# A decoder layer on one core: who makes the first product's scales, and in what order ScalarE and VectorE work within one of its blocks

## The chip, the cores and the metric

The kernel runs on one core of one Trainium2 chip. The metric is device time in microseconds (us) of one execution. Small values are better. TensorE (PE in the profile) multiplies matrices, VectorE (DVE) and ScalarE (ACT) work elementwise, GpSimd (POOL) sums over partitions, and nearly all loads are issued in order by SyncE's queue (SP).

## The reference, cut to what matters

```python
mod = (silu(c) @ w_ada + b_ada).reshape(B, 6, D)          # c: (1, 2048), w_ada: (2048, 6*2048)
sh1, sc1, gt1, sh2, sc2, gt2 = mod[:, j]                   # one row of 2048 each
h = rmsnorm(x, g_norm_mix) * (1.0 + sc1) + sh1             # x: (1, 512, 2048)
proj = h @ w_in                                            # w_in: (2048, 5120)
q, k, v, xr, xg = split(proj, 1024 columns each)
o_attn = stick_breaking_attention(q, k, v)                 # 8 heads of 128
o_lru  = rg_lru(conv(xr)) * gelu(xg)
x = x + gt1 * (concat(rmsnorm(o_attn), rmsnorm(o_lru)) @ w_out)
h = rmsnorm(x, g_norm_mlp) * (1.0 + sc2) + sh2
x = x + gt2 * (square(relu(h @ w_mlp_in)) @ w_mlp_out)     # hidden width 8192
return rmsnorm(x, g_norm_final)
```

All tensors are float32. The change lies in the first lines: silu(c), sc1 and the product that makes xr.

## The kernel before

**Layout.** x is kept transposed: 16 blocks `xs[k]` of 128 channels by 512 tokens. Every float32 product is done as three single-pass products in the format `float32r`: an operand is split into a high part `h` (a ScalarE copy into `float32r`) and a low part `lo` (VectorE: full minus high, in the helper `low`, line 123), and `mm3` (lines 266, 269, 270) adds high weights by high x, high weights by low x and low weights by high x.

**Before the first product.** The row c is loaded in two halves. The first half is broadcast by the load itself to all 128 partitions of `cb[0]` (512 KB written, 4 KB read 128 times). The second half lands on one partition (`crow`), and two matmuls in full float32 with a column of ones (line 182) put it on all partitions. ScalarE applies Silu to each. 12 matmuls into an unused bank follow (`WARM`, line 186).

**Modulation rows.** A row of `mod` for channel block j of kind m (`Rows.row(m, j)`) is a dot product of 128 rows of `w_ada` with silu(c): two tiles of 128x1024 are loaded, and VectorE makes one multiply pass over each that also adds up (line 216; each is followed by a short read of the accumulator). For the first product's kind `SC1`, VectorE then adds the two sums and the bias (line 225, into `mods`), and makes the scale gm1[k] = (sc1 + 1) * g_norm_mix (line 387).

**The first product** makes xr: for k = 0..15 it multiplies x[k] * gm1[k] with two 512-column halves of `w_in`, accumulating in all 8 PSUM banks, 24 matmuls of 512 columns for each k. The rsqrt factor of the norm and the shift are applied later, so the product can start before the sum of squares is known. Block k is prepared one k ahead: `weights1(k+1)` loads two weight halves into `wr` (4 buffers) and splits them, `load_x(k+j)` loads x of a later block and squares it (ScalarE), adding the square to `acc` (VectorE, line 369), and `prep1(k+1)` makes the row, the scale and the split of the scaled x: high on ScalarE (line 390), low on VectorE (line 391). When all 16 squares are in `acc`, GpSimd sums them over partitions (`rnorm_steps`, line 343), and ScalarE and VectorE make the rsqrt factor `r1` (lines 352 to 361).

**The second product** (q, k and v of two and four heads) uses the full norm: `prep2(k)` needs the row `SH1` of block k, `r1`, and splits again (lines 397, 399, 400). It needs the same 8 banks; ScalarE first copies the first product's results out of them (line 459).

**Order.** A scheduler orders each engine's instructions by priority, raised for some by `tc.high_priority(offset=...)`; instructions given to `later` (`tc.keep_in_program_order`) stand among each other in program order. All engines run their lists strictly in order.

Of the kernel before, what the change touches and what calls it, by code (L numbers as in the profile page):

```python
# [10 lines left out]
F32 = mybir.dt.float32  # L11
# [32 lines left out]
PAD, SHIFT = 8, 16  # L44
WARM = 12

# [19 lines left out]
def hybrid_layer_kernel(  # L66
# [87 lines left out]
    def triangles():  # L154
# [20 lines left out]
    crow = T("tt")  # L175
    nc.sync.dma_start(crow[0:1, :1024], c[:, 1024:])
    nc.sync.dma_start(cb[0], c[:, :1024].broadcast_to([P, 1024]))
    act(cb[0], cb[0], AF.Silu)
    for i in range(2):
        v = slice(i * S, (i + 1) * S)  # L180
        ps = bank("mm")
        later(mm(ps, ones[0:1, :], crow[0:1, v], start=True, stop=True))
        act(cb[1][:, v], ps, AF.Silu)
    warm = bank("o")
# [6 lines left out]
    class Rows:  # L191
# [15 lines left out]
        def row(self, m, j, tags, q=None):  # L207
# [4 lines left out]
            for q_ in (0, 1) if q is None else (q,):  # L212
                if (i, q_) not in self.tiles:
                    self.load(2, tags)
                t = self.tiles.pop((i, q_))
                ins = stt(
                    out=t, in0=t, scalar=1.0, in1=cb[q_], op0=ALU.mult, op1=ALU.mult, accum_out=self.ga[:, q_ : q_ + 1],
                )
                if q is not None or tags is MID:
                    later(ins)  # L220
                del t
                if tags is not MID:
                    self.load(1, tags)
            if q != 0:
                stt(
                    out=mod(m, j), in0=self.ga[:, 0:1], scalar=self.ga[:, 1:2], in1=col(C_BADA, i), op0=ALU.add, op1=ALU.add,
                )
# [109 lines left out]
    def rnorm(*args):  # L337
        return list(rnorm_steps(*args))[1]

    def rnorm_steps(accs, n, ptag, tok=slice(0, S), r=None):  # L340
        m = T("n")[:, tok]
# [14 lines left out]
        if ptag is None:  # L356
            later(ins)
        act(r, r, AF.Exp, scale=-0.5)
        tt(out=m, in0=m, in1=r, op=ALU.mult)
# [14 lines left out]
    xs, xhl, hT = {}, {}, {}  # L374

    def load_x(k):
        xs[k] = T("a")
        with tc.high_priority(offset=XPRI):
            ins = nc.sync.dma_start(xs[k], xT[blk(k), :])
            if k == 0:  # L380
                later(ins)
        add_square(acc, xs[k], T("n"), k == 0)

    def prep1(k, tags):
        rows.row(SC1, k, tags)
        g = gm1[:, k : k + 1]
        stt(out=g, in0=mod(SC1, k), scalar=1.0, in1=col(C_GMIX, k), op0=ALU.add, op1=ALU.mult)
        h, lo = T("a", F32R), T("a", F32R)
        with tc.high_priority(offset=RPRI if k > NK - 4 else 0):
            act(h, xs[k], AF.Copy, scale=g)  # L390
            stt(out=lo, in0=xs[k], scalar=g, in1=f32(h), op0=ALU.mult, op1=ALU.subtract)
        xhl[k] = h, lo

    def prep2(k):
        rows.row(SH1, k, EARLY)
        t = xs[k]
        stt(out=t, in0=t, scalar=gm1[:, k : k + 1], in1=r1, op0=ALU.mult, op1=ALU.mult)
        h, lo = T("a", F32R), T("a", F32R)
# [24 lines left out]
    load_x(0)  # L423
    w = weights1(0, [0])
    prep1(0, None)
    w += weights1(0, [1])
    load_x(1)
    rows.load(2, EARLY)
    for k in range(NK):
        if k + 1 < NK:  # L430
            w_next = weights1(k + 1)
            for j in (2,) if k < 4 else (2, 3) if k == 4 else (3,) if k < 8 else (3, 4) if k == 8 else (4,):
                if k + j < NK:
                    load_x(k + j)
# [1049 lines left out]
def _layout(inputs):  # L1484
# [39 lines left out]
```

## Time and profile before

| | |
|---|---|
| median of 3 runs | 1973.74 us (1971.24 to 1974.24) |
| the profiled execution, its own time | 1972.66 us |
| its span from first to last instruction | 1970.9 us |
| mean granted TensorE clock | 0.997 |
| busy over the span: PE, DVE, ACT, POOL | 98%, 89%, 54%, 10% |
| first matmul of the first product | 11.82 us after the span's start |
| first matmul of the second product | 106.38 us |

The profile is of one execution, with all times from the span's start. Start to start, successive 512-column matmuls stand 0.23 us apart at full clock, so a block of 24 takes 5.44 us; a matmul's own row says 0.39 us because matmuls overlap in the pipeline. An idle time in a row is that of the engine just before it, with the instruction that ended the wait. In the window tables the last three columns are the granted clock of TensorE, the mean busy share of the 16 DMA engines and the rate in GB/s.

### The profile page before, as it was taken

The numbers are of one execution on the slowest core, as the hardware profiler recorded it, in microseconds if no ns is written. First come the engines' busy times: TensorE is split into PE (matmuls) and PEld (weight loads), VectorE is DVE, ScalarE is ACT, GpSimd is POOL, SyncE is SP. The second block draws the span as 40 slices with busy tenths as digits, with TensorE's granted clock in tenths as the row PEclk, the third lists the DMA queues.
The fourth block names the chain that finished last, engine by engine and source line by source line (L and its number), as shares of the span: only waits on it lengthen the run. The fifth ranks groups of instructions, "written<-read, shape, count | busy, mean of one in ns | idle before, by whom it ended". The sixth has DMA issues, their size and how long they took to land. (4 is left out here: it accounts for less than half of the span.)

```text
span 1970.9 us, 37264 instructions
## 1 busy us (share of the span) xinstructions
PE 1936.0 (98%) x14184; PEld 1816.2 (92%) x14184; DVE 1756.5 (89%) x2972; ACT 1067.9 (54%) x1575; POOL 203.4 (10%) x325
## 2 busy tenths in 40 slices
PE   9999999999999999999999999999999999999997
PEld 7788888788888999999999999999999999999996
DVE  8998777878998589999999999999989879879897
ACT  4443564786533376565565555556445545646452
POOL 0000000000000001112112111200001210311110
PEclk9999999999999999999999999999999999999999
DMA  9987647545879545556656666765678668669553
GB/s 366 328 293 236 205 132 230 177 129 182 290 248 372 180 144 177 188 185 225 204 178 218 206 193 193 232 209 174 226 276 288 249 244 280 224 247 356 205 198 113
DMA packets 204086, 443.51 MB, mean 225 GB/s; under 512 B 20481, under 2 KB 42113, under 8 KB 203906
## 3 DMA queue, kind: packets, MB, share of 16 engines
q1 hardware_dynamic: 176338, 356.58, 54.5%
q0 software_dynamic: 25120, 82.33, 11.3%
q8 instruction: 111, 1.82, 0.4%
q10 hardware_dynamic: 2448, 2.21, 0.3%
q14 instruction: 69, 0.57, 0.1%
HBM read 376.30 MB, written 64.75 MB: 224 GB/s over the span
## 5 line engine op out<-in xcount | busy, mean ns | idle before, releaser
L1144 PE MATMUL ps_mm<-a,w 128*128 128x256 f32 x1680 | 463.3, 276 | 2.4 <-DVE a L1164 1.8
L1146 PE MATMUL ps_mm<-a,w 128*128 128x256 f32 x1680 | 464.0, 276 | 0.3 <-DVE w L123 0.3
L1145 PE MATMUL ps_mm<-a,w 128*128 128x256 f32 x1680 | 463.7, 276 | 0.3 <-DVE a L123 0.3
L1082 ACT ACTIVATE w<-raw 128x768 fp32r<-128x768 f32 x242 | 203.6, 842 | 297.7 <-issue 97.8
L1145 PE MATMUL ps_z<-a,w 128*128 128x256 f32 x1292 | 356.9, 276 | 0.9 <-DVE a L123 0.9
L1146 PE MATMUL ps_z<-a,w 128*128 128x256 f32 x1292 | 356.7, 276 | 0.2 <-DVE w L123 0.2
L1144 PE MATMUL ps_z<-a,w 128*128 128x256 f32 x1292 | 356.7, 276 | 0.1
L123 DVE TENSOR_TENSOR w<-ts,w 128x1024 fp32r<-128x1024 f32 x242 | 295.2, 1220 | 59.4 <-PE ps_z L1146 21.6
L1088 ACT ACTIVATE w<-ts 128x1024 fp32r<-128x1024 f32 x242 | 256.1, 1058 | 156.7 <-DVE ts L1084 141.1
L1144 PEld LDWEIGHTS ps_mm<-a,w 128*128 128x128 f32 x1680 | 315.0, 188 | 3.1 <-issue 2.9
L1146 PEld LDWEIGHTS ps_mm<-a,w 128*128 128x128 f32 x1680 | 315.4, 188 | 0.9 <-DVE w L123 0.9
L1145 PEld LDWEIGHTS ps_mm<-a,w 128*128 128x128 f32 x1680 | 315.4, 188 | 0.5 <-DVE a L123 0.5
L123 DVE TENSOR_TENSOR w<-raw,w 128x768 fp32r<-128x768 f32 (+2 forms) x296 | 267.5, 905 | 26.6 <-ACT w L249 23.1
L1145 PEld LDWEIGHTS ps_z<-a,w 128*128 128x128 f32 x1292 | 242.5, 188 | 1.4 <-DVE a L123 1.3
L1146 PEld LDWEIGHTS ps_z<-a,w 128*128 128x128 f32 x1292 | 242.5, 188 | 0.4 <-DVE w L123 0.4
L1144 PEld LDWEIGHTS ps_z<-a,w 128*128 128x128 f32 x1292 | 242.6, 188 | 0.2 <-ACT a L1203 0.2
L249 ACT ACTIVATE wh<-wr 128x512 fp32r<-128x512 f32 (+1 forms) x184 | 112.8, 617 | 138.7 <-PE ps_mm L269 73.1
L266 PE MATMUL ps_mm<-a,wh 128*128 128x512 f32 x448 | 175.5, 392 | 2.2 <-DVE a L471 1.2
L270 PE MATMUL ps_mm<-a,wl 128*128 128x512 f32 x448 | 174.4, 390 | 0.7 <-DVE wl L123 0.6
L269 PE MATMUL ps_mm<-a,wh 128*128 128x512 f32 x448 | 174.6, 390 | 0.0
L1076 DVE TENSOR_TENSOR ts<-raw 128x512 f32<-128x512 f32 x242 | 165.2, 683 | 8.0 <-DMA raw<-in_w_mlp_out_dram 7.7
L123 DVE TENSOR_TENSOR wl<-wr,wh 128x512 fp32r<-128x512 f32 (+1 forms) x184 | 123.2, 673 | 35.8 <-ACT wh L249 32.8
(359 smaller groups left out, 4068.5 us busy)
## 6 DMA issues: line engine op xcount, KB each, us to landing
raw<-in_w_mlp_out_dram SPq DMA_DIRECT2D x124, 512.0 KB, 4.4
raw<-in_w_mlp_in_dram SPq DMA_DIRECT2D x120, 512.0 KB, 3.8
x<-in_w_adaT_dram SPq DMA_DIRECT2D x108, 512.0 KB, 5.8
wr<-in_w_in_dram SPq DMA_DIRECT2D x160, 256.0 KB, 4.0
tt<-in_w_adaT_dram SPq DMA_DIRECT2D x52, 512.0 KB, 6.5
part<-a POOLq DMA_DIRECT2D x84, 256.0 KB, 4.1
a<-part SPq DMA_DIRECT2D x84, 256.0 KB, 6.2
n<-in_w_adaT_dram SPq DMA_DIRECT2D x64, 256.0 KB, 4.2
```

What stands on the lines that cost most here:

```text
L123: return tt(out=out, in0=full, in1=f32(high), op=ALU.subtract)
L249: ins = act(h[:, :n], r[:, :n], AF.Copy), low(lo[:, :n], r[:, :n], h[:, :n])
L266: first = mm(out, wh, ah, start=start, stop=False, **kw)
L269: mm(out, wh, al, start=False, stop=False, **kw)
L270: mm(out, wl, ah, start=False, stop=stop, **kw)
L1076: tt(out=t[:, : 2 * HT].rearrange("p (a b) -> p a b", a=2), in0=r[:, HT : 3 * HT].rearrange("p (a b) -> p a b", a=2), in1=r[:, q_(0)].unsq ...
L1082: act(h, r[:, HT:], AF.Copy)
L1088: act(h, t, AF.Copy)
L1144: mm(out, wh[:, blk(i)], ah, start=st, stop=False, **kw)
L1145: mm(out, wh[:, blk(i)], al, start=False, stop=False, **kw)
L1146: mm(out, wl[:, blk(i)], ah, start=False, stop=j == js[-1], **kw)
```

## The change

The first product is rearranged; past the second product no engine's order differs.

- **c.** The host lays c out 128 times in memory, and the load of `cb[0]` reads 128 different rows. The second half is broadcast by four single-pass `float32r` matmuls (high and low part of each 512 columns) in place of two full float32 ones. ScalarE makes the high parts and a `float32r` copy of the ones, VectorE the low parts. There are 9 warming matmuls, not 12.
- **Scales.** VectorE still makes the two multiply passes of a row `SC1`. ScalarE then adds the two sums (line 238 of the new file) and makes the scale from it with one more instruction (line 439), using `gb` = (bias + 1) * g_norm_mix, which is made once for all 16 blocks.
- **Order within a block.** Nearly all instructions of a block are given to `later`. ScalarE: high parts of the two weight halves, the square, the two short ones for the scale, high part of x. VectorE: the two passes of the row, the add of a square, low parts of the weights, low part of x. The adds of squares come in `add_squares`, all done by block 13; the sum over partitions is issued after block 13's preparation, one block later than before.
- **Row SH1 of block 0** is made after block 15 is prepared (it was made partly before). `triangles()`, which makes constants with GpSimd, moves from the end of the product to block 2.

On ScalarE, from the first table load on (`cb` is silu(c), `ps_mm` the banks of the broadcast, `n` a square, `a` every 128x512 tile), stood before:

```order
L1475 ACT_TABLE_LOAD
L183 ACTIVATE cb_82<-ps_mm_103 128x512
L178 ACTIVATE cb_81<-cb_81 128x1024
L183 ACTIVATE cb_82<-ps_mm_106 128x512
L1475 ACT_TABLE_LOAD
L366 ACTIVATE n_122<-a_135 128x512
L249 ACTIVATE a_141<-wr_139 128x512
L390 ACTIVATE a_150<-a_135,gm_77 128x512
```

and on the same engine at the same place there stands now:

```order
L186 ACTIVATE a_105<-tt_100 1x512
L186 ACTIVATE a_109<-tt_100 1x512
L193 ACTIVATE cb_82<-cb_82 128x1024
L195 ACTIVATE cb_83<-ps_mm_113 128x512
L195 ACTIVATE cb_83<-ps_mm_114 128x512
L1532 ACT_TABLE_LOAD
L407 ACTIVATE n_133<-a_146 128x512
L425 ACTIVATE a_150<-wr_149 128x512
L238 ACTIVATE ga_158<-ga_158 128x1
L439 ACTIVATE gm_77<-ga_158,gb,vec 128x1
L440 ACTIVATE a_162<-a_146,gm_77 128x512
```

Both Silus of the second half now follow that of the first half, and two short instructions stand ahead of the scaled x.

On VectorE, the preparation of block 5 (`x` and `tt` hold tiles of `w_ada`, `wr` the weights, `n` the squares) was:

```order
L216 SCALAR_TENSOR_TENSOR tt_296,ga_348<-tt_296,cb_81 128x1024
L216 SCALAR_TENSOR_TENSOR x_299,ga_348<-x_299,cb_82 128x1024
L225 SCALAR_TENSOR_TENSOR mods<-ga_348,vec 128x1
L123 TENSOR_TENSOR a_334<-wr_331,a_333 128x512
L387 SCALAR_TENSOR_TENSOR gm_77<-mods,vec 128x1
L123 TENSOR_TENSOR a_340<-wr_337,a_339 128x512
L391 SCALAR_TENSOR_TENSOR a_358<-a_289,gm_77,a_357 128x512
L369 TENSOR_TENSOR n_122<-n_122,n_345 128x512
```

and is now, for a block of the same length:

```order
L228 SCALAR_TENSOR_TENSOR tt_313,ga_365<-tt_313,cb_82 128x1024
L228 SCALAR_TENSOR_TENSOR x_316,ga_365<-x_316,cb_83 128x1024
L415 TENSOR_TENSOR n_133<-n_133,n_363 128x512
L124 TENSOR_TENSOR a_353<-wr_351,a_352 128x512
L124 TENSOR_TENSOR a_358<-wr_356,a_357 128x512
L444 SCALAR_TENSOR_TENSOR a_374<-a_307,gm_77,a_373 128x512
```

The two short instructions are gone, and the add of the square stands ahead of the splits.

On VectorE, at the end of the first product (`a_962` in the first piece and `a_976` in the second are the low part of x of block 15; `a_975` before and `a_995` now that of the second product's block 0), stood before:

```order
L216 SCALAR_TENSOR_TENSOR x_908,ga_1008<-x_908,cb_81 128x1024
L359 TENSOR_TENSOR n_794<-n_794,n_896 128x512
L391 SCALAR_TENSOR_TENSOR a_913<-a_735,gm_77,a_912 128x512
L360 SCALAR_TENSOR_TENSOR n_794<-n_794,n_896 128x512
L123 TENSOR_TENSOR a_943<-wr_940,a_942 128x512
L361 SCALAR_TENSOR_TENSOR n_896<-n_794,n_896 128x512
L123 TENSOR_TENSOR a_949<-wr_946,a_948 128x512
L397 SCALAR_TENSOR_TENSOR a_135<-a_135,gm_77,n_896 128x512
L391 SCALAR_TENSOR_TENSOR a_962<-a_789,gm_77,a_961 128x512
L216 SCALAR_TENSOR_TENSOR x_954,ga_1008<-x_954,cb_82 128x1024
L400 SCALAR_TENSOR_TENSOR a_975<-a_135,mods,a_974 128x512
```

and there stands now:

```order
L444 SCALAR_TENSOR_TENSOR a_976<-a_805,gm_77,a_975 128x512
L228 SCALAR_TENSOR_TENSOR x_866,ga_982<-x_866,cb_82 128x1024
L228 SCALAR_TENSOR_TENSOR tt_916,ga_982<-tt_916,cb_83 128x1024
L228 SCALAR_TENSOR_TENSOR x_919,ga_1028<-x_919,cb_82 128x1024
L240 SCALAR_TENSOR_TENSOR mods<-ga_982,vec 128x1
L228 SCALAR_TENSOR_TENSOR x_969,ga_1028<-x_969,cb_83 128x1024
L460 SCALAR_TENSOR_TENSOR a_995<-a_146,mods,a_994 128x512
L124 TENSOR_TENSOR wl_1001<-wr_998,wh_1000 128x512
L124 TENSOR_TENSOR wl_1117<-wr_1114,wh_1116 128x512
L124 TENSOR_TENSOR wl_1148<-wr_1145,wh_1147 128x512
L240 SCALAR_TENSOR_TENSOR mods<-ga_1028,vec 128x1
L455 SCALAR_TENSOR_TENSOR a_170<-a_170,gm_77,n_963 128x512
```

Between the last low part of the first product and the first of the second, one pass over a `w_ada` tile stood before, and four stand now. On ScalarE at that place, the scaled and shifted x of the second product's block 1 (`a_1037`, made from `a_170`) still stands ahead of the copies out of the banks:

```order
L459 ACTIVATE a_994<-a_146,mods 128x512
L268 ACTIVATE wh_1000<-wr_998 128x512
L268 ACTIVATE wh_1116<-wr_1114 128x512
L268 ACTIVATE wh_1147<-wr_1145 128x512
L459 ACTIVATE a_1037<-a_170,mods 128x512
L517 ACTIVATE a_1065<-ps_mm_134 128x512
```

where before it was:

```order
L399 ACTIVATE a_974<-a_135,mods 128x512
L249 ACTIVATE wh_980<-wr_978 128x512
L399 ACTIVATE a_1017<-a_160,mods 128x512
L249 ACTIVATE wh_1106<-wr_1104 128x512
L249 ACTIVATE wh_1137<-wr_1135 128x512
L459 ACTIVATE a_1045<-ps_mm_123 128x512
```

One weight copy has changed places with it.

The diff, cut to its core:

```diff
-WARM = 12
+WARM = 9
+RPRI = 250
...
-    nc.sync.dma_start(cb[0], c[:, :1024].broadcast_to([P, 1024]))
+    nc.sync.dma_start(cb[0], c[:, :1024])
+    ones_r = T("a", F32R)[0:1, :P]
+    act(ones_r, ones[0:1, :], AF.Copy)
+    crows = []
+    for i in range(2):
+        v, h, lo = crow[0:1, i * S : (i + 1) * S], T("a", F32R)[0:1, :], T("a", F32R)[0:1, :]
+        act(h, v, AF.Copy)
+        low(lo, v, h)
+        crows.append((h, lo))
+    ps = [bank("mm"), bank("mm")]
+    for q in range(2):
+        for i in range(2):
+            later(mm(ps[i], ones_r, crows[i][q], start=q == 0, stop=q == 1))
     act(cb[0], cb[0], AF.Silu)
     for i in range(2):
-        v = slice(i * S, (i + 1) * S)
-        ps = bank("mm")
-        later(mm(ps, ones[0:1, :], crow[0:1, v], start=True, stop=True))
-        act(cb[1][:, v], ps, AF.Silu)
+        act(cb[1][:, i * S : (i + 1) * S], ps[i], AF.Silu)
...
-            if q != 0:
+            if m == SC1:
+                with tc.high_priority(offset=RPRI):
+                    later(act(self.ga[:, 2:3], self.ga[:, 0:1], AF.Identity, bias=self.ga[:, 1:2]))
+            elif q != 0:
                 stt(out=mod(m, j), in0=self.ga[:, 0:1], scalar=self.ga[:, 1:2], in1=col(C_BADA, i), ...)
...
-    def prep1(k, tags):
+    def prep1(k, tags, made, first):
         rows.row(SC1, k, tags)
         g = gm1[:, k : k + 1]
-        stt(out=g, in0=mod(SC1, k), scalar=1.0, in1=col(C_GMIX, k), op0=ALU.add, op1=ALU.mult)
         h, lo = T("a", F32R), T("a", F32R)
+        with tc.high_priority(offset=RPRI):
+            later(act(g, rows.ga[:, 2:3], AF.Identity, bias=gb[:, k : k + 1], scale=col(C_GMIX, k)))
+            later(act(h, xs[k], AF.Copy, scale=g))
+        add_squares(0 if k == 0 else NK if k == NK - 3 else k + 1)
+        w = lows(k, made[:first])
         with tc.high_priority(offset=RPRI if k > NK - 4 else 0):
-            act(h, xs[k], AF.Copy, scale=g)
-            stt(out=lo, in0=xs[k], scalar=g, in1=f32(h), op0=ALU.mult, op1=ALU.subtract)
+            later(stt(out=lo, in0=xs[k], scalar=g, in1=f32(h), op0=ALU.mult, op1=ALU.subtract))
...
-            w_next = weights1(k + 1)
+            made = halves(k + 1)
...
-            if k + 4 == NK - 1:
-                    r1_gen = rnorm_steps([acc], D, None)
-                    next(r1_gen)
-            if k + 2 == NK - 1:
-                    r1 = next(r1_gen)
-            prep1(k + 1, EARLY)
             if k + 1 == NK - 1:
                 with tc.high_priority(offset=RPRI):
+                    next(r1_gen)
+            w_next = prep1(k + 1, EARLY, made, 2)
+            if k + 3 == NK - 1:
+                    r1_gen = rnorm_steps([acc], D, None, pin=True)
+                    next(r1_gen)
+            if k + 1 == NK - 1:
+                with tc.high_priority(offset=RPRI):
+                    rows.row(SH1, 0, EARLY)
+                    r1 = next(r1_gen)
                     prep2(0)
```

More of the change, by code (lines that the diff above doesn't have):

```diff
@@ L218, in row @@
                 )
-                if q is not None or tags is MID:
+                if q is not None or tags is MID or m == SC1 or m == SH1 and j == 0:
                     later(ins)
@@ L227, in row @@
                 )
+    stt(
+        out=gb, in0=vec[:, C_BADA + SC1 * NK : C_BADA + (SC1 + 1) * NK], scalar=1.0, in1=vec[:, C_GMIX : C_GMIX + NK],
+        op0=ALU.add, op1=ALU.mult,
+    )
     rows, rows2 = Rows(SC1, SH1), Rows(GT1, SC2, SH2)
@@ L357, in rnorm_steps @@
             later(ins)
-        act(r, r, AF.Exp, scale=-0.5)
+        ins = act(r, r, AF.Exp, scale=-0.5)
+        if pin:
+            later(ins)
+        yield
         tt(out=m, in0=m, in1=r, op=ALU.mult)
@@ L381, in load_x, with add_squares, halves @@
                 later(ins)
-        add_square(acc, xs[k], T("n"), k == 0)
-    def prep1(k, tags):
+        if k == 0:
+            act(acc, xs[k], AF.Square)
+        else:
+            q = T("n")
+            act(q, xs[k], AF.Square)
+            squares.append((k, q))
+    def add_squares(k):
+        while squares and squares[0][0] <= k:
+            later(tt(out=acc, in0=acc, in1=squares.pop(0)[1], op=ALU.add))
+    def halves(k):
+        made = []
+        with tc.high_priority(offset=min(max(k - 1, 0) * 28, URGENT)):
+            for i in range(2):
+                r, h, lo = T("wr"), T("a", F32R), T("a", F32R)
+                later(nc.sync.dma_start(r, w_in[blk(k), XR + i * S : XR + (i + 1) * S]))
+                made.append((h, lo, r))
+                if k or i == 0:
+                    later(act(h, r, AF.Copy))
+        return made
@@ L385, in prep1, with lows @@
+    def lows(k, made):
+        with tc.high_priority(offset=min(max(k - 1, 0) * 28, URGENT)):
+            for h, lo, r in made:
+                later(low(lo, r, h))
+        return [(h, lo) for h, lo, _ in made]
+    def prep1(k, tags, made, first):
         rows.row(SC1, k, tags)
         g = gm1[:, k : k + 1]
-        stt(out=g, in0=mod(SC1, k), scalar=1.0, in1=col(C_GMIX, k), op0=ALU.add, op1=ALU.mult)
         h, lo = T("a", F32R), T("a", F32R)
+        with tc.high_priority(offset=RPRI):
[3 more added lines that the diff above has]
+        w = lows(k, made[:first])
@@ L389, in prep1 @@
         with tc.high_priority(offset=RPRI if k > NK - 4 else 0):
-            act(h, xs[k], AF.Copy, scale=g)
-            stt(out=lo, in0=xs[k], scalar=g, in1=f32(h), op0=ALU.mult, op1=ALU.subtract)
+            later(stt(out=lo, in0=xs[k], scalar=g, in1=f32(h), op0=ALU.mult, op1=ALU.subtract))
         xhl[k] = h, lo
+        if made[first:]:
+            wh, _, r = made[first]
+            later(act(wh, r, AF.Copy))
+        return w + lows(k, made[first:])
     def prep2(k):
-        rows.row(SH1, k, EARLY)
+        if k:
+            rows.row(SH1, k, EARLY)
@@ L396, in prep2 @@
         t = xs[k]
[L397 removed]
+        ins = stt(out=t, in0=t, scalar=gm1[:, k : k + 1], in1=r1, op0=ALU.mult, op1=ALU.mult)
+        if k < 3:
+            later(ins)
         h, lo = T("a", F32R), T("a", F32R)
```

30 lines of the change are left out of this document (14 added, 16 removed).

## The prediction

> **What bounds the kernel now.** I read first the window table by stage, then who waited for whom on TensorE in the first 104 us, then TensorE's timeline there.
>
> ```profile
> 5.00:11.80 6.80, 6.19 (x26) 4.60 (x24) 3.46 (x8) 5.13 (x8) 0.28 (x1) 1.00 1.04 387
> 11.80:104.00 92.20, 87.90 (x374) 71.06 (x375) 90.49 (x173) 41.06 (x70) 4.57 (x3) 0.98 0.94 348
> 104.00:190.00 86.00, 86.00 (x381) 71.23 (x380) 79.27 (x140) 33.71 (x56) 0.00 (x0) 1.00 0.78 266
> ...
> PE ps_mm L269 <- DVE a L391: 4.0, 4, 2.4
> PE ps_mm L182 <- DMA tt<-in_c_dram: 2.7, 1, 2.7
> ```
>
> In the first product TensorE is busy 87.9 of 92.2 us and VectorE 90.5, so both are near their limit. What TensorE waits for is mostly the low part of x (L391), which VectorE makes. In the second product TensorE is never idle, so time gained ahead of it should reach the end of the kernel, unless a new wait takes it.
>
> ```profile
> 11.82 0.50 PE L266 MATMUL ps_mm<-a,a 128*128 128x512 f32 x1 [0.62 <-ACT a L390]
> ...
> 23.97 0.39 PE L266 MATMUL ps_mm<-a,a 128*128 128x512 f32 x1
> ...
> 62.67 0.39 PE L266 MATMUL ps_mm<-a,a 128*128 128x512 f32 x1
> ...
> 69.44 0.39 PE L266 MATMUL ps_mm<-a,a 128*128 128x512 f32 x1
> ...
> 80.32 0.39 PE L266 MATMUL ps_mm<-a,a 128*128 128x512 f32 x1
> ...
> 85.76 0.39 PE L266 MATMUL ps_mm<-a,a 128*128 128x512 f32 x1
> 88.54 0.59 PE L269 MATMUL ps_mm<-a,a 128*128 128x512 f32 x1 [2.39 <-DVE a L391]
> ...
> 95.50 1.07 PE L266 MATMUL ps_mm<-a,a 128*128 128x512 f32 x4
> ...
> 106.38 0.39 PE L266 MATMUL ps_mm<-a,wh 128*128 128x512 f32 x1
> ```
>
> The rows are first matmuls of blocks 0, 2, 9, 10, 12, 13 and 14, and of the second product; 88.54 is block 13's second. A block without a wait takes 85.76 - 80.32 = 5.44 us. Sixteen would take 87.0, but 11.82 to 106.38 is 94.56, so 7.5 us are lost: 23.97 - 11.82 less two blocks is 1.27 in blocks 0 and 1; 62.67 - 23.97 less seven is 0.62; block 9 loses 69.44 - 62.67 - 5.44 = 1.33; block 13 loses 95.50 - 85.76 - 5.44 = 4.30. Of the last only 2.39 is the wait. The clock has the rest:
>
> ```profile
> 85.40:88.80 3.40, 1.01 (x5) 0.55 (x4) 3.40 (x7) 2.59 (x6) 0.06 (x1) 1.00 0.27 90
> 88.80:92.20 3.40, 3.40 (x9) 2.63 (x9) 3.37 (x8) 1.87 (x3) 0.00 (x0) 0.50 0.89 272
> ```
>
> After a stretch with TensorE busy 1.01 of 3.40 us, 3.40 us run at clock 0.50, so 1.7 us are lost.
>
> **Block by block, VectorE.** One block before, and what delayed block 13:
>
> ```profile
> 65.36 1.22 DVE L216 SCALAR_TENSOR_TENSOR tt<-tt,cb 128x1024 f32<-128x1024 f32 x1
> 66.50 0.08 DVE L216 DVE_READ_ACCUMULATOR tt<-tt,cb 128x1 f32 x1
> 66.50 1.22 DVE L216 SCALAR_TENSOR_TENSOR x<-x,cb 128x1024 f32<-128x1024 f32 x1
> 67.65 0.09 DVE L216 DVE_READ_ACCUMULATOR x<-x,cb 128x1 f32 x1
> 67.77 0.22 DVE L225 SCALAR_TENSOR_TENSOR mods<-ga,vec 128x1 f32<-128x1 f32 x1
> 67.91 0.68 DVE L123 TENSOR_TENSOR a<-wr,a 128x512 fp32r<-128x512 f32 x1
> 68.51 0.15 DVE L387 SCALAR_TENSOR_TENSOR gm<-mods,vec 128x1 f32<-128x1 f32 x1
> 68.58 0.68 DVE L123 TENSOR_TENSOR a<-wr,a 128x512 fp32r<-128x512 f32 x1
> 69.18 0.74 DVE L391 SCALAR_TENSOR_TENSOR a<-a,gm,a 128x512 fp32r<-128x512 f32 x1
> 69.84 0.68 DVE L369 TENSOR_TENSOR n<-n,n 128x512 f32<-128x512 f32 x1
> 70.44 1.22 DVE L216 SCALAR_TENSOR_TENSOR tt<-tt,cb 128x1024 f32<-128x1024 f32 x1
> ...
> 80.82 4.11 POOL L343 PARTITION_ALL_REDUCE n<-n  x1 [69.69 <-DVE n L369]
> ...
> 81.75 3.25 DVE L216 SCALAR_TENSOR_TENSOR tt<-tt,cb 128x1024 f32<-128x1024 f32 x1
> 85.40 1.21 DVE L216 SCALAR_TENSOR_TENSOR x<-x,cb 128x1024 f32<-128x1024 f32 x1
> ```
>
> Start to start, a pass takes 1.14 us, a low part or an add 0.60, L391 0.66; the block 70.44 - 65.36 = 5.08. The two short instructions with the gap ahead of them take 0.33, and they go: the new block is 2.29 + 0.60 + 1.20 + 0.66 = 4.75 us. Against 5.44 on TensorE, VectorE gains 0.69 a block. Before, it spent such slack on rows not needed yet (the pass at 85.40, ahead of block 13's splits); the fixed order forbids that, so the slack becomes a lead of the low part over TensorE. Beside the sum over partitions a pass takes 3.25 instead of 1.22, a loss of 2.0 us, and the new order keeps that sum, one block later.
>
> **ScalarE.** In a block it has two weight copies, a square, two short instructions and L440. I price a short one by 208 ns of this 128x8 row, and L440 as L390's 0.71:
>
> ```profile
> L535 ACT ACTIVATE spe<-spe 128x8 f32<-128x8 f32 x1 | 0.2, 208 | 0.0
> ```
>
> From the row's end to h: two times 0.22 and 0.71, about 1.2 us with a hop. VectorE has 1.8 us of add and weight splits in that time, so the moved scale is hidden. If that cover is gone (blocks 14, 15 have no add) it costs 0.1. The short instructions would cost nothing at the low end, and at the high end as much as a copy (0.63 each), which would make VectorE wait 0.2 a block; still under 5.44. The square is queued ahead of the scale, so an x that lands late holds h back; that decides block 1.
>
> **The start.**
>
> ```profile
> 2.00:5.00 3.00, 2.27 (x3) 1.16 (x4) 0.17 (x1) 0.70 (x2) 0.00 (x0) 1.00 1.01 205
> ...
> 6.64 1.06 ACT L178 ACTIVATE cb<-cb 128x1024 f32<-128x1024 f32 x1 [1.24 <-DMA cb<-in_c_dram]
> 7.61 0.58 ACT L183 ACTIVATE cb<-ps_mm 128x512 f32<-128x512 f32 x1
> 8.20 1.28 ACT L1475 ACT_TABLE_LOAD   x1
> 9.86 0.63 ACT L366 ACTIVATE n<-a 128x512 f32<-128x512 f32 x1 [0.37 <-DMA a<-in_xT_dram]
> 10.52 0.63 ACT L249 ACTIVATE a<-wr 128x512 fp32r<-128x512 f32 x1
> 11.06 0.71 ACT L390 ACTIVATE a<-a,gm 128x512 fp32r<-128x512 f32 x1
> ...
> 7.98 1.23 DVE L216 SCALAR_TENSOR_TENSOR x<-x,cb 128x1024 f32<-128x1024 f32 x1 [4.85 <-DMA x<-in_w_adaT_dram]
> ...
> 9.85 0.33 SPq L379 DMA_DIRECT2D a<-in_xT_dram  x1
> ...
> a<-in_xT_dram SPq DMA_DIRECT2D x1, 256.0 KB, 7.0
> ```
>
> The DMA engines are full in both windows (1.01, 1.04), but move 205 GB/s from 2 to 5 us and 387 after. In those 3 us it is mostly c, one 4 KB piece read 128 times. If 128 separate pieces move like w_ada's, c and all later loads land 3.0 * (387 - 205) / 387 = 1.4 us earlier. Bounds: 0 (the slowness is the queues' start) and 1.5; I take 1.4, because the rate recovers when c's bytes are done (3.0 us of 205 GB/s is 0.6 MB, c and the other two small loads).
>
> On ScalarE then: c at 5.2, Silu to 6.2, two Silus of 0.58 to 7.4, table to 8.7, square, copy to 9.95, two short ones, L440 10.4 to 11.1. The second half of c landed at 2.7 (the wait row of L182 at the top); two high parts of 0.6, a low part of 0.7 and a last matmul of 0.5 (L266's first row) put the broadcast at 5.1, hidden under c's load at either end of that price. So the first matmul comes at 11.1, 0.7 earlier; without a faster c it would be 12.5, 0.65 later, since two Silus and the square now stand in front.
>
> Block 1 is decided by x of block 2. Its load, issued at 9.85, landed at 16.85; now 15.45. Its square ends at 16.1, h of block 1 at 17.3, and on VectorE the add, two splits and L444 follow to 16.1 + 0.6 + 1.2 + 0.66 = 18.6. TensorE does three high matmuls ahead of the first low one, 0.68 us, so block 1 counts from 18.6 - 0.68 = 17.9, and no later block waits: block 2 needs its low part at 17.9 + 5.44 + 1.36 (six high ones first now) = 24.7 and has it at 18.6 + 4.75 = 23.35. The second product starts at 17.9 + 15 * 5.44 = 99.5 instead of 106.38: 6.9 us earlier.
>
> **The second product's start** is where this could be given back. VectorE's lead: low part 12 comes at 18.6 + 11 * 4.75 = 70.85. Block 13 has two adds and the sum over partitions: 2.29 + 1.2 + 1.2 + 0.66 + 2.0 = 7.35. Block 14 takes 4.15. Block 15 has five more instructions of the rsqrt and prep2 chain, four of 0.6 to 0.66 and a short one of about 0.4: 7.0. So low part 15 is there at 89.35; block 15 starts at 17.9 + 14 * 5.44 = 94.05, a lead of 4.7 us. From there VectorE has four passes, the low part, three weight splits, two short ones and L455: 4.58 + 0.66 + 1.8 + 0.27 + 0.66 = 8.0; then ScalarE's L459 of block 1 (0.7) and the first copy out of a bank (0.6): the bank is free 9.3 us after low part 15, and TensorE wants it at 4.7 + 5.44 = 10.1. So 0.8 us to spare, and no wait. I take 0.3 off for what such a walk misses: 6.9 - 0.3 = 6.6 us.
>
> The loads go in the same order on SP's queue, whose waits for a free `wr` buffer come from the same splits; a block moves 2 * 0.52 + 3 * 0.26 = 1.84 MB, which at 387 GB/s is 4.75 us: just VectorE's pace. The four broadcast matmuls, `gb` and the two low parts of c are hidden under c's load; `triangles()`, two short copies on ScalarE, in its idle half.
>
> **Sum.** The profiled execution's own time is 1972.66, its span 1970.9, and the median of the runs is 1973.74, 1.1 above. 1972.66 - 6.6 = 1966.1; against the median 1967.1. I forecast 1966.8. 0.2%, about what a measurement of this kernel can tell from no change, is 3.9 us here.
>
> **Rivals.**
> - *c is no faster.* The start is 0.65 late, but x of block 2 then lands at 16.85 as before, and block 1 counts from 19.3: 5.5 - 0.3 = 5.2 us gained, 1968.0. For it: first transfers may just be slow. Against: the recovery at c's end. Chance 0.15.
> - *The lead is too short.* If VectorE's pace is 5.0 instead of 4.75 (weights landing late, short instructions dearer), 11 blocks cost 2.75 of the lead; the first bank is free 2 us late, and a gap like block 13's takes 1.7 us of clock too: 3.2 gained, about 1969.5. Against: ScalarE's half-idle block. Chance 0.19.
> - *The sum over partitions blocks VectorE for its whole 4.11 us*, not 2.0 of it. That leaves a lead of 2.6, and the bank 1.3 us late: 5.3 gained, 1967.9. The row speaks against it: the pass at 81.75 ended 3.25 later. The Trainium skill (SBUF — State Buffer, Who interferes with whom) has the port pair that VectorE and GpSimd share as an exclusive lock, held for a whole instruction. By that rule 4.11 would be lost; this trace shows half. Chance 0.04.
> - *The clock's 1.7 us stay.* If the half-speed stretch after 88.8 was not due to the gap, 4.9 are gained, 1968.2. The Trainium skill (TensorE: Matmul & The Clock Gate, HAM oscillation) warns of idle gaps over about 3.4 us, and this one was 2.39; the row of 1.01 busy in 3.40 says a shorter one is enough. Chance 0.04.
> - *Slower.* Weights arrive late in every block. A `wr` buffer is loaded again after the split two blocks earlier; in the strict order, issue (0.4), landing, copy (0.65) and split (0.7) must fit into two blocks. With 7.0 landing it is 8.75 against 9.5. Landing beyond 2 * 5.44 - 1.75 = 9.1 us stops TensorE every block, and beyond 10.1 (5.91 a block, the average before) the kernel is slower; at 10.8 by 16 * 0.35 = 5.6, 1979. Before, rows done ahead filled such waits. Against: the rate of 348 GB/s shows reserve below 387. Chance 0.08.
>
> **How the numbers follow.** My case (1965.3 to 1968.5, for the lead and the run spread) has 0.50. Its ceiling is a start at 11.1 with no wait at all, 8 us gained and 1964.5. Faster by over 0.2% (below 1969.8) holds in my case, the first, third and fourth rival and half of the second, less 0.02 for the run spread: 0.80. Same is the other half of the second with that 0.02, 0.12; slower 0.08. For eight in ten I go from just past the ceiling, 1964.0, to 1970.8, where most of the second rival is in.
>
> **What would show it.** In the changed profile: TensorE's rows free of waits for L444 after block 1, no stretch of clock 0.50, block starts 5.44 apart; first matmul near 11.1; first copy out of a bank before the second product's first matmul, near 99.5; the window 2 to 5 us near 390 GB/s. Waits of VectorE's L124 for ScalarE's L425 would show the slower case; a gap ahead of the second product's first matmul, the short lead.

## The result: 26 us slower, lost where the change altered no instruction

The changed kernel takes 1999.39 us (median of 4 runs, 1998.75 to 1999.93) against 1973.37 for the kernel before: a ratio of 1.0133 [1.0116, 1.0151]. The forecast was 1966.8.

From 768 us to 1930 us (1957 us in the changed kernel) runs the main part of the MLP: 10,164 matmuls of 256 columns in one helper, three lines of it, the same instructions in the same order in both kernels. Two of its groups on the page, before and then after (busy time, mean ns of one):

```profile
L1144 PE MATMUL ps_mm<-a,w 128*128 128x256 f32 x1680 | 463.3, 276 | 2.4 <-DVE a L1164 1.8
L1145 PE MATMUL ps_z<-a,w 128*128 128x256 f32 x1292 | 356.9, 276 | 0.9 <-DVE a L123 0.9
```

```profile
L1201 PE MATMUL ps_mm<-a,w 128*128 128x256 f32 x1680 | 468.0, 279 | 0.6 <-DVE a L1221 0.5
L1202 PE MATMUL ps_z<-a,w 128*128 128x256 f32 x1292 | 361.7, 280 | 0.7 <-DVE a L124 0.7
```

Same counts, hardly a wait, but 3 to 4 ns more for each. A window of 100 us in which TensorE is never idle shows the rate (first before, then after; the first pair is PE's busy time and its matmuls):

```profile
1000.00:1100.00 100.00, 100.00 (x885) 100.00 (x884) 97.62 (x163) 53.67 (x69) 19.20 (x29) 1.00 0.66 212
```

```profile
1000.00:1100.00 100.00, 100.00 (x861) 100.00 (x860) 96.26 (x162) 52.53 (x68) 20.31 (x30) 1.00 0.67 210
```

885 against 861 matmuls, at full clock in both. Start to start, a matmul stands 113 or 114 ns behind the one before it in the kernel before, nearly always; after, 112 to 124 ns. From the first of these matmuls to the last it takes 1162.4 us before and 1189.2 after: **26.8 us**, nearly all of the 26.95 between the two profiled executions. The steps alone make more, about 31 us (those under 150 ns are 113.4 ns on average before and 116.5 after), because the short waits between them are 5 us less after.

The front part, which the prediction was about, did what its mechanism said, and gave most of it back. TensorE's waits in the first 130 us, and the place where the second one falls, on TensorE and then ScalarE:

```profile
PE ps_mm L192 <- ACT a L186: 3.4, 1, 3.4
PE ps_mm L285 <- ACT a L440: 2.8, 1, 2.8
PE ps_mm L285 <- ACT a L517: 2.7, 1, 2.7
...
104.12 0.50 PE L285 MATMUL ps_mm<-a,wh 128*128 128x512 f32 x1 [2.70 <-ACT a L517]
...
102.86 0.72 ACT L459 ACTIVATE a<-a,mods 128x512 fp32r<-128x512 f32 x1 [2.12 <-DVE a L455]
103.49 2.04 ACT L517 ACTIVATE a<-ps_mm 128x512 f32<-128x512 f32 x4
...
105.90:109.30 3.40, 3.40 (x11) 2.70 (x10) 3.40 (x7) 2.84 (x6) 0.00 (x0) 0.59 0.91 324
```

Block 1 starts at 19.66, then each block 5.44 later without a wait for the low part of x: block 15 stands at 95.82, and the second product could start at 101.26, 5.1 us earlier than before. But ScalarE holds the high part of the second product's next x (L459) ahead of the copies that free the banks (L517) and waits for it; TensorE waits 2.70 us, and then 3.41 us of the second product's block 0 run at half clock, from 105.26 to 108.67 (mean 0.59 in the window above). Block 1 of the second product starts at 111.31, where before it started at 111.81: 0.5 us are left.

### The profile page after: what moved, and what is told of

It reads as the page before. It is cut to its first block, busy times and chain, and to the rows that moved or that the text cites. A ratio compares the mean times of both kernels' runs of the same rounds, so it can differ in the third digit from the quotient of the medians.

```text
span 1997.9 us, 37265 instructions
## 1 busy us (share of the span) xinstructions
PE 1966.7 (98%) x14178; PEld 1849.8 (93%) x14178; DVE 1754.9 (88%) x2943; ACT 1082.7 (54%) x1610; POOL 202.8 (10%) x325
## 5 line engine op out<-in xcount | busy, mean ns | idle before, releaser
L1202 PE MATMUL ps_mm<-a,w 128*128 128x256 f32 x1680 | 469.9, 280 | 0.1
L1201 PE MATMUL ps_mm<-a,w 128*128 128x256 f32 x1680 | 468.0, 279 | 0.6 <-DVE a L1221 0.5
L1203 PE MATMUL ps_mm<-a,w 128*128 128x256 f32 x1680 | 467.6, 278 | 0.0
L1202 PE MATMUL ps_z<-a,w 128*128 128x256 f32 x1292 | 361.7, 280 | 0.7 <-DVE a L124 0.7
L1201 PE MATMUL ps_z<-a,w 128*128 128x256 f32 x1292 | 360.7, 279 | 0.0
L1203 PE MATMUL ps_z<-a,w 128*128 128x256 f32 x1292 | 359.4, 278 | 0.0
```

Of the source, the lines that this page charges most:

```text
L1201: mm(out, wh[:, blk(i)], ah, start=st, stop=False, **kw)
L1202: mm(out, wh[:, blk(i)], al, start=False, stop=False, **kw)
L1203: mm(out, wl[:, blk(i)], ah, start=False, stop=j == js[-1], **kw)
```

## What in the change slows the MLP

The change makes one new tile: `gb`, 16 columns of float32, in the pool `top`, which grows from the right end of SBUF.

```diff
-    mods, gm1, spl = (top.tile(...) for n, t in ((96, "mods"), (NK, "gm1"), (HEADS, "spl")))
+    mods, gm1, gb, spl = (top.tile(...) for n, t in ((96, "mods"), (NK, "gm1"), (NK, "gb"), (HEADS, "spl")))
```

Every later tile on the right side lies 64 bytes lower for it, among them `w4`, one of three pools (`w3`, `w4`, `w5`) from which the MLP's matmuls read weights. Theory 'place': those 64 bytes are the loss. Rival: something else in the change is. First the changed kernel moved by a further 64 bytes, then the kernel before moved by 64, 128 and 32, by an unused tile alone:

```diff
     mods, gm1, gb, spl = (...)
+    top.tile([P, 16], F32, tag="gap", name="gap")     # 32 or 8 columns in the other runs
```

> The changed kernel with an unused 16-column tile behind `gb`, so that every tile on the right side of SBUF lies 128 bytes below its place in the kernel before, not 64; order of every engine unchanged. Theory 'place' (the 64 bytes of `gb` slow the matmuls of the MLP by 26.8 us, about 2.6 ns each): these matmuls go back to a step of 113 to 114 ns and the time to 1999.4 - 26.8 = 1972.6 us (1970 to 1975), if a multiple of 128 bytes is enough; if only 256 does it, it stays above 1985. Rival 'rest of the change' (order of ScalarE and VectorE, c, the clock): nothing moves, 1998 to 2001.

> The kernel before with an unused 16-column tile (64 bytes) in the same pool; nothing else of the change, order of every engine unchanged. Theory 'place': 1973.4 + 26.8 = 2000 us (1996 to 2003), with a step of 116 ns in the MLP's 256-column matmuls. Rival 'rest of the change': 1973 as before (1971 to 1975).

> The kernel before with an unused 32-column tile (128 bytes). Theory 'place': no change if the rule goes by 128 bytes, 1973.4 (1971 to 1975); 1985 or more if it goes by 256. Rival 'rest of the change': 1973 too; that a gap by itself costs something (less room, another place) would show as a slower time here.

> The kernel before with an unused 8-column tile (32 bytes). Theory 'place', to find its grain: if a place off a multiple of 64 costs at least as much as one off 128, 2000 us or more; if a row of 512 bytes simply touches one piece more, the same 2000; if 32 bytes were the grain, 1973. Rival 'rest of the change': 1973.

Before took 1972.0 here. With 64 bytes it takes 2001.4 (1.0144 [1.0129, 1.0160]) with nothing else of the change: the theory stands, and the rival falls. 32 bytes cost more, 2006.8 (1.0174 [1.0159, 1.0189]). My guess for 128 bytes was wrong in both directions: neither fast nor slow, but spread from run to run, 1975.4 to 1994.7 for the kernel before and 1973.7 to 2003.0 for the changed one. Two windows of the one trace with 128 bytes show why:

```profile
1000.00:1100.00 100.00, 100.00 (x885) 100.00 (x884) 98.14 (x165) 53.99 (x69) 19.65 (x29) 1.00 0.66 211
1600.00:1700.00 100.00, 100.00 (x852) 100.00 (x851) 83.87 (x124) 56.68 (x79) 15.75 (x29) 1.00 0.78 271
```

From 890 to 1280 us the step averages 113.33 ns, from 1400 to 1870 us 117.78 ns, with no step of the other pace in either. There are two paces, and the step changes between them behind a short wait of TensorE (a step of about 180 to 230 ns), in both directions: behind the wait at 1877 us it is 113.3 ns again.

**Operand or bystander.** `ts` and `raw`, which these matmuls do not read (only the elementwise engines and DMAs do in this stage), moved too. Two layouts of that pool part them:

```diff
-    "sums": ("right", {"ts": 2, "raw": 3, "w4": 4}),
+    "sums": ("right", {"w4": 4, "gap": 1, "ts": 2, "raw": 3}),   # only w4 is moved by 64
+    "sums": ("right", {"ts": 2, "raw": 3, "gap": 1, "w4": 4}),   # only ts and raw are
```

> The kernel before, with only the pool of the MLP's stage laid out anew: `w4` first and 64 bytes lower than a multiple of 256 (192 over one), `ts` and `raw` (the full-precision sums and loads that only the elementwise engines and the DMAs touch) at multiples of 256 as before. Theory 'operand of the matmul' (TensorE itself is slower when it reads weights from there): 2000 us (1990 to 2004). Rival 'elementwise or DMA side' (writes of `raw` and reads of `ts` disturb TensorE from their new place): 1972, no change.

> The counterpart: `ts` and `raw` 64 bytes lower (192 over a multiple of 256), `w4` where it was in the kernel before. Theory 'operand of the matmul': 1972 us, no change (1970 to 1975). Rival 'elementwise or DMA side': 2000.

2000.6 (1.0139 [1.0125, 1.0153]) and 1973.4 (1.0002 [0.9992, 1.0011]): it is the weights' place as TensorE reads it.

**Which place.** I thought of multiples of 256 bytes. Moving `w3` and `w5` there, and moving only `a`, the operand that streams past the weights:

```diff
-PAD, SHIFT = 8, 16
+PAD, SHIFT = 8, 48      # first run: w3, w5 at 0
+PAD, SHIFT = 24, 16     # second run, with the tile "shift" left out: a at 128
```

> The kernel before, with the unused tile `shift` 48 columns wide instead of 16, so that `w3` and `w5` start at multiples of 256 as `w4` does (before: 128 over one); order unchanged. Theory 'multiple of 256' (weights at a multiple of 256 bytes are the fast ones, and those at 128 are carried along): 1972 us in every run (1970 to 1975). Rival 'neighbours must differ' (what helps is that `w4` and `w3`, loaded in turn, lie 128 bytes apart over 256): as with all three at 128 over 256, a time that varies from run to run between 1973 and 2005.

> The kernel before, with `pad` 16 columns wider and `shift` left out, so that `a` (the moving operand of the MLP's matmuls) starts 128 over a multiple of 256, not 64, with `w3`, `w4` and `w5` where they were; `n`, `cb`, `wr`, `wh` and `wl` of the front move by 64 bytes too. Theory 'place of the weights': 1972 us, the MLP's step stays at 113.3 ns. Rival 'place of the weights against the moving operand': `w4` is then 128 over `a`, as in the changed kernel, and the time is near 2000.

2010.9 (1.0189 [1.0175, 1.0203]) and 2022.1 (1.0249 [1.0232, 1.0266]): both theories fall. With all weights at multiples of 256 TensorE keeps the slow pace, 117.78 ns, to 1890 us, and the time is 2009 to 2012 in every run, not spread as the rival had it; and with every weight where it had been, moving `a` costs 49 us, more than that rival's 27. So a weight's place by itself doesn't decide it, and the distance between the operands may. The last two runs test that:

```diff
-    mods, gm1, spl = (top.tile(...) for n, t in ((96, "mods"), (NK, "gm1"), (HEADS, "spl")))
+    gm1 = const(NK, "gm1"); mods, spl = (...)            # first run: all operands 64 higher
-    "mlp": ("left", {"shift": 1, "w5": 1, "w3": 6}),
+    "mlp": ("left", {"w5": 1, "w3": 6}),                 # second run: w3, w5 at 64
```

> The kernel before, with the small tile `gm1` on the left side of SBUF instead of the right, so that all operands of the MLP's matmuls lie 64 bytes higher: `a` at 128 over a multiple of 256, `w4` at 64, `w3` and `w5` at 192; order unchanged. Theory 'places against each other' (only the distance between weights and moving operand counts): 1972 us, the step stays at 113.3 ns. Rival 'place by itself': with `a` at 128 as in the run of 2022.1 us, 1990 to 2022.

> The kernel before without the unused tile `shift`, so that `w3` and `w5` start 64 bytes over a multiple of 256, as `a` does, and `w4` at 0 as before; order unchanged. Theory 'the two weight pools need 128 between them': slow, 1990 to 2020. Rival 'any difference will do': 1972. Rival 'weights must not start where the moving operand does, modulo 256': slow too, and the steps on `w3` are the longer ones.

All moved together: 1972.5, 0.9998 [0.9989, 1.0008], no change. `w3` at the same place as `a`: 2006.0, 1.0162 [1.0146, 1.0179]; the median step of a matmul with weights in `w3` is 120 ns, with weights in `w4` (or `w5`, one tile in five) 114 ns, as the last rival has it. That the two pools need 128 between them doesn't explain the run of 2022.1 us, where they have it. So the distance between the weights and the moving operand counts. The windows of 1000 to 1100 us of the last four runs, in the order told:

```profile
1000.00:1100.00 100.00, 100.00 (x852) 100.00 (x851) 95.45 (x160) 52.91 (x69) 20.32 (x30) 1.00 0.65 208
```

```profile
1000.00:1100.00 100.00, 100.00 (x843) 100.00 (x842) 94.43 (x156) 54.56 (x73) 19.00 (x28) 1.00 0.62 197
```

```profile
1000.00:1100.00 100.00, 100.00 (x884) 100.00 (x884) 97.68 (x162) 53.68 (x70) 18.95 (x28) 1.00 0.68 212
```

```profile
1000.00:1100.00 100.00, 100.00 (x856) 100.00 (x855) 95.61 (x161) 53.60 (x70) 20.33 (x30) 1.00 0.65 207
```

All together, with the distances from the start of `a`'s tiles in bytes, modulo 256 (from the addresses of each build):

| `w4` - `a` | `w3`, `w5` - `a` | us | matmuls in 100 us |
|---|---|---|---|
| 192 | 64 (before; also all moved by 64) | 1972 to 1973 | 885, 884 |
| 128 | 64 (the changed kernel; also before with 64 bytes) | 1999 to 2001 | 861 |
| 160 | 64 | 2006.8 | 857 |
| 64 | 64 | 1973.7 to 2003.0 | 885 or 852 |
| 192 | 192 | 2010.9 | 852 |
| 192 | 0 | 2006.0 | 856 |
| 128 | 0 | 2022.1 | 843 |

Of these only 192 with 64 holds 113.33 ns. Distances of 0, 128 and 160 give irregular long steps; 64 alone goes back and forth between the two paces, 192 alone holds the slow one. Other distances were not tried, and what in the memory does this isn't shown. What VectorE and ScalarE do in the meantime isn't the cause: with both idle for the whole step, the changed kernel's steps are 115.6 ns on average (241 of them, 800 to 1900 us) against 116.5 overall and 113.4 in the kernel before. The Trainium skill (SBUF — State Buffer, Who interferes with whom) gives TensorE two independent read ports, for the moving operand and for the weights, and has it wait on no one. On "independent" these runs don't agree: with every weight in its place, the kernel takes 2.5% longer when only the moving operand (and, in the front part, tiles that the MLP's matmuls don't read) lies 64 bytes higher.

## The front part, with the operands back in place

The change no longer uses 16 columns of `mods`; `gb` fits there, and nothing moves. On top of that, in the second run the high and low part of the second product's block 1 are written behind the copies of the banks:

```diff
+    gb = mods[:, SC1 * NK : (SC1 + 1) * NK]
...
         else:
-            prep2(1)
+            prep2(1, 1)          # row and scaled x
...
     for o in range(8):
         act(t, banks[o], AF.Copy)
+    prep2(1, 2)                  # its high and low part
```

> The changed kernel with `gb` kept in the 16 columns of `mods` that the change leaves unused, so that every tile lies where it lay in the kernel before; nothing else. Theory 'place': the matmuls of the MLP step by 113.3 ns again and all 26.8 us come back; the front part is worth only the 0.5 us by which block 1 of the second product starts earlier, so the ratio to before is 0.9997 (0.999 to 1.0005), about 1971.5 where before has 1972.0. Rival 'rest of the change': still 1.013. Rival 'my forecast was right but for the place': 1965, a ratio of 0.9965; the wait of 2.7 us for the copy out of a bank and the second half-speed stretch speak against it.

> As the one with `gb` in `mods`, and the high and low part of the second product's block 1 are written behind the copies of the banks in the program, so that ScalarE frees the banks before it waits for that x. Theory 'bank freed late': the wait of 2.7 us and the half-speed stretch behind it (1.7 us) go, the second product starts near 101.4 and its block 1 near 107: 4.4 us less than the one with `gb` in `mods`, a ratio to before of 0.9975. Rival 'the wait moves': block 1 then waits for its low part, which VectorE makes later, 1 to 3 us, and half the gain is given back; rival 'loads': the second product runs into its weights and all of it is given back, 0.9997.

The first gives 0.9992 [0.9983, 1.0001]: from 1.0133, 27.8 us come back, and the rest of the change is worth about 1.6 us, not 6.6; the interval only just includes no gain at all. The second gives 1967.0, 0.9970 [0.9959, 0.9982], 4.3 us more. How that divides between the wait and the clock isn't shown: in the one trace of the first the wait was 1.71 us and no half-speed stretch followed it, and block 1 of the second product started at 108.89. The second's waits of TensorE and its ScalarE at that place (the lines of the new code stand 7 further down):

```profile
...
PE ps_mm L285 <- ACT a L440: 2.3, 1, 2.3
PE ps_mm L288 <- DVE a L444: 0.4, 1, 0.4
...
97.51 1.66 ACT L268 ACTIVATE wh<-wr 128x512 fp32r<-128x512 f32 x3
99.08 2.03 ACT L524 ACTIVATE a<-ps_mm 128x512 f32<-128x512 f32 x4
100.98 1.58 ACT L524 ACTIVATE a<-ps_z 128x512 f32<-128x512 f32 x3
...
103.91 0.72 ACT L466 ACTIVATE a<-a,mods 128x512 fp32r<-128x512 f32 x1
```

The copies start at 99.08 instead of 103.49, the second product at 100.20 without a wait, and block 1 at 105.64. The rival "the wait moves" did not come.

From this version, one part of the change at a time was undone:

```diff
-    nc.sync.dma_start(cb[0], c[:, :1024])
+    nc.sync.dma_start(cb[0], c[0:1, :1024].broadcast_to([P, 1024]))      # first run
...
-                    later(act(self.ga[:, 2:3], self.ga[:, 0:1], AF.Identity, bias=self.ga[:, 1:2]))
+                later(stt(out=mod(m, j), in0=self.ga[:, 0:1], scalar=self.ga[:, 1:2], ...))     # second run
-            later(act(g, rows.ga[:, 2:3], AF.Identity, bias=gb[:, k : k + 1], scale=col(C_GMIX, k)))
+            later(stt(out=g, in0=mod(SC1, k), scalar=1.0, in1=col(C_GMIX, k), ...))
```

> The version with the copies of the banks first (1967.0 us, a ratio of 0.9970), with the first half of c loaded from one row again, read 128 times, as in the kernel before. The forecast's term 'c 1.4 us earlier': all loads behind c land 1.0 to 1.4 us later, block 1 and with it the second product start that much later, 1968.0 to 1968.4, a ratio of 0.9976. Rival 'c no faster': 0.9970, and the rate from 2 to 5 us stays near 240 GB/s.

> The version with the copies of the banks first, with the sum of the row and the scale made by VectorE again (two short instructions behind the two passes, in the fixed order), ScalarE without them. The forecast's term 'VectorE 0.33 us a block': its block is 5.08 instead of 4.75 us, 15 blocks use up 5 us of a lead that is 1 to 2.5 us at block 15, so TensorE waits 2.5 to 4 us by the end of the first product: 1969.5 to 1972.5, a ratio of 0.9982 to 0.9998. Rival 'the lead is set by the loads' (the lost leads of 1.4 and 1.2 us were weights that came late): no difference, 0.9970.

*c by one row*: 1968.2, 0.9973 [0.9962, 0.9984], which the times can't tell from 0.9970. The traces can, one of each: the Silu of c, with 128 rows and with one,

```profile
5.46 1.06 ACT L193 ACTIVATE cb<-cb 128x1024 f32<-128x1024 f32 x1 [1.61 <-DMA cb<-in_c_dram]
```

```profile
5.88 1.06 ACT L193 ACTIVATE cb<-cb 128x1024 f32<-128x1024 f32 x1 [2.03 <-DMA cb<-in_c_dram]
```

so the layout is worth 0.4 us, not the 1.4 of the forecast.

*Scale on VectorE*: 1971.1, 0.9988 [0.9979, 0.9997], 3.5 us slower by the ratios, and within the range expected. VectorE's block there, from one low part of x to the next:

```profile
44.48 0.74 DVE L445 SCALAR_TENSOR_TENSOR a<-a,gm,a 128x512 fp32r<-128x512 f32 x1
...
47.55 0.22 DVE L237 SCALAR_TENSOR_TENSOR mods<-ga,vec 128x1 f32<-128x1 f32 x1
47.80 0.16 DVE L440 SCALAR_TENSOR_TENSOR gm<-mods,vec 128x1 f32<-128x1 f32 x1
...
49.69 0.74 DVE L445 SCALAR_TENSOR_TENSOR a<-a,gm,a 128x512 fp32r<-128x512 f32 x1
```

5.21 us against 4.76 in the changed kernel (its L444 at 23.57 and 28.33); and TensorE waits again, 0.6 us for the low part of x and 1.6 for the first bank. This part of the change does what it was forecast to do, 0.45 us a block where the forecast had 0.33.

**The clock at the start.** The last run has 14 warming matmuls instead of 9, on the version with the copies first.

> The version with the copies of the banks first (1967.0 us, 0.9970), with 14 warming matmuls instead of 9; each takes 0.47 us, so TensorE's idle time ahead of the first product shrinks from 2.3 to 2.9 us to about 0.3. Theory 'the gap drops the clock': no stretch of clock 0.50 at 13 to 17 us in any trace; where it appeared it cost block 1 about 0.8 us, so the time is 1966.2 to 1967.0, a ratio of 0.9966 to 0.9970. Rival 'the clock rises late whatever the gap': a half-speed stretch still; rival 'warming in the way': the first product starts later, 1967.5.

1965.9, 0.9963 [0.9950, 0.9976]: not to be told from 0.9970 by time, and its second product starts at 100.22, as without them. Its trace has no half-speed stretch, but the one with 9 warming matmuls has none either, so the run doesn't part the theory from its rivals. The length of a gap alone does not decide it. Here are a gap of 2.38 us with a half-speed stretch behind it (scale on VectorE), one of 2.33 without (copies first), and one of 2.39 without (the version with `w3` at the place of `a`, ahead of block 13):

```profile
11.47 1.88 PE L286 MATMUL ps_mm<-a,a 128*128 128x512 f32 x4 [2.38 <-ACT a L441]
...
8.32:11.73 3.41, 1.03 (x8) 0.84 (x7) 3.05 (x8) 2.75 (x5) 0.44 (x2) 1.00 1.05 413
11.73:15.14 3.41, 3.41 (x9) 2.64 (x9) 3.41 (x5) 1.21 (x3) 0.00 (x0) 0.50 1.04 413
```

```profile
12.02 1.20 PE L285 MATMUL ps_mm<-a,a 128*128 128x512 f32 x4 [2.33 <-ACT a L440]
...
10.38:13.79 3.41, 1.77 (x8) 1.47 (x9) 2.48 (x4) 2.56 (x6) 0.74 (x2) 1.00 1.03 412
13.79:17.20 3.41, 3.41 (x17) 2.82 (x16) 3.22 (x7) 2.64 (x6) 0.29 (x1) 1.00 1.04 419
```

```profile
88.17 0.50 PE L269 MATMUL ps_mm<-a,a 128*128 128x512 f32 x1 [2.39 <-DVE a L391]
...
83.55:86.96 3.41, 2.23 (x10) 1.50 (x8) 3.34 (x8) 3.38 (x7) 1.47 (x3) 1.00 0.50 201
86.96:90.37 3.41, 2.20 (x10) 1.82 (x11) 3.41 (x7) 0.60 (x2) 0.00 (x0) 1.00 0.58 184
90.37:93.78 3.41, 3.41 (x17) 2.83 (x16) 3.38 (x11) 1.27 (x3) 0.00 (x0) 1.00 0.89 288
```

In each trace the records of the granted clock start a whole number of 3.41 us apart, and the windows above are cut at these places. The first gap lies within one such stretch, which has 2.38 us idle; the third falls into two, with 1.2 us idle in each. Over all 17 traces, from the first record of the clock on and the idle end of the kernel aside, ten stretches have 2.12 to 2.78 us idle, and each is followed by one at half clock; no stretch has between 1.79 and 2.12, and none with 1.79 or less is followed by one. Where these stretches begin differs from execution to execution: in ten traces of the kernel before and its other layouts the gap of 2.4 us ahead of block 13 cost half-speed time in five. So 1.7 us more or less can be chance in one trace. (Ahead of its first record the clock's column says 1.00, but the rate isn't full there: in the kernel before, whose first record is at 10.30, the warming matmuls step by 0.21 us up to there and by 0.11 us after it.)

This version has the lowest median, 7 us below the kernel before.

## Why the prediction was wrong, step by step

**The step that failed** is "the four broadcast matmuls, `gb` and the two low parts of c are hidden under c's load". I priced `gb` as an instruction, not as 64 bytes that move everything beside it, and took the MLP's time as given because no engine's order there differs. None of my rivals had it; the slower one was about weights loaded late. Between 1966.1, the forecast for the profiled execution, and its 1999.6 lie 33.5 us: 26.8 are the MLP's matmuls, 6.1 the front part (6.6 forecast, 0.5 there), and about 0.6 lies between block 1 of the second product and the MLP (655.8 us before, 656.5 after), for a reason that isn't shown. The front part's terms:

**The start**, forecast 11.1, was 12.46, and block 1 counted from 19.66 instead of 17.9: 1.8 us. c landed 1.0 us earlier than before, not 1.4, and its layout made 0.4 of that; the two short instructions take 0.73 us (0.31 and 0.42 start to start), not 0.44; x, not ScalarE, held the square:

```profile
9.75 0.63 ACT L407 ACTIVATE n<-a 128x512 f32<-128x512 f32 x1 [0.80 <-DMA a<-in_xT_dram]
10.41 0.63 ACT L425 ACTIVATE a<-wr 128x512 fp32r<-128x512 f32 x1
10.95 0.28 ACT L238 ACTIVATE ga<-ga 128x1 f32<-128x1 f32 x1
11.26 0.39 ACT L439 ACTIVATE gm<-ga,gb,vec 128x1 f32<-128x1 f32 x1
11.68 0.72 ACT L440 ACTIVATE a<-a,gm 128x512 fp32r<-128x512 f32 x1
...
13.80:17.20 3.40, 3.40 (x11) 2.69 (x10) 3.09 (x6) 2.09 (x5) 0.29 (x1) 0.60 1.05 411
```

and behind a gap of 2.79 us, 3.41 us of the first block ran at half clock, which the forecast had not asked about. For block 1 this was nearly all of it: in the two traces without such a stretch (copies first, and 14 warming matmuls) block 1 starts at 17.81 and 17.75, as forecast.

**The lead of VectorE**, forecast 4.7 us at block 15, was 1.0. The pace was right (4.76 where I had 4.75), and so was the way from low part 15 to the free bank: 9.3 us, as forecast (94.8 to 104.1). The lead was lost to weights that came late, twice:

```profile
35.25 1.30 ACT L425 ACTIVATE a<-wr 128x512 fp32r<-128x512 f32 x2 [2.37 <-DMA wr<-in_w_in_dram]
36.58 1.30 ACT L410 ACTIVATE n<-a 128x512 f32<-128x512 f32 x2
...
37.25 0.69 DVE L415 TENSOR_TENSOR n<-n,n 128x512 f32<-128x512 f32 x1 [1.12 <-ACT n L410]
...
59.56 0.75 DVE L444 SCALAR_TENSOR_TENSOR a<-a,gm,a 128x512 fp32r<-128x512 f32 x1 [1.16 <-ACT a L440]
...
87.62 0.43 DVE L374 TENSOR_SCALAR n<-n 128x512 f32<-128x512 f32 x1 [0.90 <-ACT n L371]
```

Each time ScalarE has two squares queued behind the late copies, and VectorE, in its fixed order, waits for what comes after them: 1.4 and 1.2 us over a block's pace. The DMA engines were full there (1.06 and 1.05 busy from 33 to 36 and from 53 to 56 us, at 394 and 393 GB/s). That is the load's own limit, which I had worked out (4.75 us a block) and called "just VectorE's pace", where a pace without reserve means that each late piece is lost for good. Block 15 lost a further 1.1, most of it in the wait for ScalarE's L371, a step of the rsqrt, and 0.9 were missing from block 1 on. So low part 15 came 5.4 us late and TensorE only 1.8. With a lead of 1.0 the bank is 2.86 us late. My rival "the lead is too short" named this place, the gap and the clock, and by its own price, 3.2 gained, was still too mild.

**The sum over partitions** cost what was forecast. Beside its 3.48 us two weight splits took 3.33 us instead of 1.28, so 2.05 were lost, not 3.48:

```profile
78.13 3.33 DVE L124 TENSOR_TENSOR a<-wr,a 128x512 fp32r<-128x512 f32 x2
```

**The clock's 1.7 us** were regained where they had been lost, because the gap there was gone, and lost twice elsewhere, in block 0 of each product. The reason that I gave, a gap, is half of it: where the gap falls in the clock's division of time decides too, and that differs from execution to execution.

## What to carry to other kernels

A tile added to a full SBUF moves the tiles beside it; where matmuls are short and TensorE never idle, compare the addresses of both matmul operands before and after any edit, and look at the step of a stage that the edit doesn't touch. When an unchanged stage takes longer with equal counts and no waits, put the tile where nothing moves before studying the rest. And a fixed order needs a reserve at each engine that feeds it: put what frees a shared buffer ahead of what can wait, or a lead won in one product is paid back at the start of the next.

## What the runs showed of the hardware that I had not expected

- The step of back-to-back 128x256 `float32r` matmuls is 113.33 ns or up to 119 ns on average by the distance modulo 256 bytes between weights and moving operand, 2.5% of the kernel's time at worst. Two pools of weights at 192 and 64 bytes from it held the fast step; 64 and 64 gave two paces, 113.33 and 117.78 ns, that changed at short waits, and times that spread by 29 us from run to run.
- TensorE's clock dropped to half for 3.41 us behind every 3.41 us stretch of the clock's own division of time in which TensorE was idle for 2.12 us or more, and behind none with 1.79 or less. So gaps of 2.37 to 2.39 us cost half-speed time in six traces and nothing in five. The Trainium skill (TensorE: Matmul & The Clock Gate, HAM oscillation) warns of gaps over about 3.4 us; none between the matmuls here was that long.
